# Forward substitution of a delta rule by finished rows, with its matrix and products in PSUM

## The chip, the cores and the metric

The kernel runs on one core of one Trainium2 chip. The metric is the device time of one execution in microseconds, as the median of several runs. The engines are named as the profile names them: PE (TensorE, the matmuls; PEld are its weight loads), DVE (VectorE), ACT (ScalarE), POOL (GpSimd) and SP (SyncE, which issues the DMAs). PSUM is the memory that PE writes its products to; SBUF is the other memory of the core.

## The reference, cut to what matters

A network of three blocks on 512 tokens of 1024 features (and 256 context tokens in the first two). The third block has, beside a dilated attention, a gated delta rule with 8 heads of 128 features, worked in 4 chunks of 128 tokens. Inside a chunk the rule needs the solution of a triangular system:

```
L[t, s] = beta_t * exp(g_t - g_s) * (k_t . k_s)     for s < t, else 0
T       = (I + L)^-1                                per head and chunk, 128 x 128
u       = T (beta v),   w = T (beta exp(g) k)
```

Here g is the running sum of the log decays. u and w then go through a scan over the four chunks of a head, which carries a state of 128 x 128.

## The kernel before, in words

The delta rule (`delta`, L1290) takes the 8 heads in two groups of four. For each group it runs five steps:

1. `delta_prep` (L1140), once for each head: loads q, k and v from a DRAM scratch, norms q and k, makes the decays, and leaves in SBUF the matrix L as `Lm` (four chunks, L1185) and the other factors. The normed keys and queries are in a tile `kq`, three buffers for all heads.
2. `delta_base` (L1200): the inverses of the 32 x 32 blocks on the diagonal of I + L. There are 4 heads x 4 chunks x 4 blocks = 64 of them. They are written to DRAM (L1207) and read back so that each block lies in a partition of its own (`Lb`, [64, 32, 32], L1209). DVE changes the sign (L1210), sets `Tb` to the unit matrix (L1212, L1213) and then works row by row: for row i, one product of row i of -L with the first i rows of T, read transposed (L1217), and one sum over the last axis, which gives row i of T (L1218). Both have i x i elements in each of 64 partitions; i runs from 1 to 31, and each instruction needs the one before it. The result goes to DRAM (L1219). `Lb`, `Tb` and the products are in buffers of `kq`.
3. `delta_merge` (L1221), for each head: loads the blocks back onto the diagonal of a 128 x 128 matrix (`Tz`, L1244), transposes it on PE (L1237), and joins 32-blocks to 64 and 128 with matmuls (L1231), DVE subtractions from PSUM (L1256) and ACT copies from PSUM (L1246, L1252, L1255, L1258).
4. `delta_scan` (L1261): the scan over the chunks, four heads side by side.
5. The norm of the outputs (L1308 to L1313).

Between the groups `fill` is called: the projections of the dilated attention, matmuls of 512 columns (L140 to L142) with weights that are loaded by SP (L127), split by ACT (L133) and POOL (L134) into two parts, and results that ACT and, where a gate is formed, DVE (L1043) take out of PSUM and SP stores (L1044). They depend on nothing in the delta rule. More projections (`fill1` in `second`, L1438) are called behind the dilated attention, which follows the delta rule.

The instructions are not run in the order of the program text. A planner goes through the whole program when it is built; each engine takes, of the instructions whose inputs are ready in its plan, the one that comes first in the text (unless a priority is changed). The times of the plan are the planner's own. So projections that stand later in the text are put between the steps of a group wherever PE would have nothing to do in the plan. On the chip each engine runs its instructions in the planned order and waits, at each, for what it needs; the DMA queue of SP likewise.

Two pools of PSUM matter. `pm` has three buffers of 512 fp32 values in each partition, tag "mm", for the projections. `ps` has five of this size, tag "sm", for all small products of the delta rule and later of the attention. Buffers of a tag are taken in turn, and a tile waits until the last reader of the buffer's former tile is done.

Of the kernel before, what the change touches and what calls it, by code (L numbers as in the profile page):

```python
# [29 lines left out]
class Group:  # L30
    """Latent (0) or context (1) tokens: residual x and split activations, both feature-major."""
# [6 lines left out]
class Tiles:  # L38
    """Feature tiles [P, 8, m], the first six in one buffer and the last two in another."""
# [14 lines left out]
class Core:  # L54
# [14 lines left out]
    def weights(self, stack, NR, NW, first=0):  # L69
        """More weight buffers for a phase: NR raw loads of 2048 columns, NW splits of 1024; first is the raw one to start at."""  # L70
        pool = stack.enter_context(self.tc.tile_pool(name=self.nm("wp"), bufs=1, reuse_waits="tile"))
        for kind, n in (("wr", NR), ("wh", NW), ("wl", NW)):
            old = self.wbufs.get(kind, [])
            self.wbufs[kind] = old + [(pool, f"{kind}{len(old) + i}") for i in range(n)]
            stack.callback(self.wbufs.__setitem__, kind, old)
        self.wi = {"wr": first - 1}
        stack.callback(self.wi.clear)

    def wt(self, kind, shape, dt=F32):
        """The next weight buffer in turn."""  # L80
# [11 lines left out]
    def exp_table(self):  # L92
        """Behind the silus traced so far, the activation table that has both exp and ln."""
# [10 lines left out]
    def feat(self, pool, g, tag):  # L104
        """Split activations of a group."""
# [3 lines left out]
    # ---------------------------------------------------------------- weights  # L109
# [13 lines left out]
    def wcols(self, w, c0, engs=None):  # L123
        """256 columns of a [1024, *] matrix as two splits [P, 8, 128]."""
# [19 lines left out]
    def gemm(self, ps, w, H, L):  # L144
        """ps[128, n] = w.T @ (H + L) over the feature tiles."""
# [9 lines left out]
    def sigm(self, out, x):  # L155
        """out = 1 / (1 + exp(-x)) with the functions of one activation table."""
# [5 lines left out]
    def vgemm(self, pt, g, i, w, cs):  # L162
        """pt[128 tokens of tile i, 256] = h.T @ w, token-major; w: two splits of four feature tiles."""
# [6 lines left out]
    def wrows(self, w, c0):  # L170
        """256 columns of a [1024, *] matrix as two splits [P, 4 * 256] of four feature tiles."""
# [4 lines left out]
    # ---------------------------------------------------------------- setup  # L176
# [21 lines left out]
    def conditions(self, ps, pp):  # L198
        """silu of the three condition vectors, feature-major."""
# [8 lines left out]
    def params(self, ps, pp):  # L208
        """Small vectors, laid feature-major by PE transposes."""
# [18 lines left out]
    def matvec(self, ps, sb, i0, w, c0, ncol, bias, dst, tag="mv"):  # L228
        """dst[p, tile, :] = (cond[i0:i0+2] @ w[:, c0:c0+ncol])[tile*128+p] + bias, feature-major; yields after each load.
        The products add up in PSUM where the tag is mv, in SBUF where its buffers are shared."""  # L230
# [26 lines left out]
    def matvec_dve(self, ps, sb, n, w, c0, bias, dst, tag):  # L257
        """The same for 2048 / n columns and the first n conditions, the products added up by VectorE; only the sums over
        the partitions are left to TensorE."""
# [37 lines left out]
    def tick(self, n=1):  # L297
        """Advance the products that run beside a phase by n loads."""
# [7 lines left out]
    def later(self, n, f, *args):  # L306
        """f traced with its priority lowered by n instructions."""
# [5 lines left out]
    # ---------------------------------------------------------------- norm  # L313
    def affine(self, g, mod, shift, scale, i):
        """Gain and shift of a modulated norm: per-partition scalars of the 8 feature tiles."""
# [4 lines left out]
    def rstd(self, out, ps, inv):  # L320
        """out = (ps * inv + eps) ** -0.5"""
# [5 lines left out]
    def norm(self, ps, groups, mods, tag="sm"):  # L327
        """H + L = modulated norm of x, split."""
# [31 lines left out]
    # ---------------------------------------------------------------- ffn  # L360
    def ffn_w(self, w_in, c):
        """256 columns each of gate and up."""
        return self.wcols(w_in, c * 256), self.wcols(w_in, FFN + c * 256)

    def ffn(self, ps, sb, groups, gates, w_in, w_out, ticks, pre):
        """x += gate * (silu(h w_gate) * (h w_up)) w_out; ticks: loads beside each of so many chunks; pre: the first ffn_w."""
# [32 lines left out]
    # ---------------------------------------------------------------- tokens in  # L399
# [46 lines left out]
class Even(Core):  # L446
    def even_setup(self, cp, ps):
# [22 lines left out]
        # lower bounds: softmax over the two layers, first row  # L470
# [25 lines left out]
    # ------------------------------------------------------------ attention  # L496
    def qk_norm(self, ps, sb, pl, pc, gain, out):
        """out[128 = two heads x 64, 768]: head norm with gain, rope on the latent columns."""
# [18 lines left out]
    def attend(self, ps, sb, q, k, vt, t, i, yq):  # L517
        """Query tile i of heads t and 4 + t."""
# [28 lines left out]
        # exponentials, their sums with the sink's  # L547
# [15 lines left out]
        # token-major products with the values  # L563
# [20 lines left out]
    # ------------------------------------------------------------ hgrn  # L584
    def hgrn_dir(self, sb, d, h, pl, pc):
        """Gates of one direction: 1 - f and the cumulative log f inside chunks of 128."""
# [13 lines left out]
    def hgrn_part(self, ps, sb, d, q, k, cum, c0, m):  # L600
# [26 lines left out]
        # keys of the half of a chunk that comes first, queries of the other, from the bound between them  # L627
# [19 lines left out]
        # scores [s, t] by blocks of 32 keys; the parts that are masked whole are left out  # L647
# [61 lines left out]
    # ------------------------------------------------------------ mixer  # L709
    def even_mixer(self, groups, ydram, side, out):  # L710
# [3 lines left out]
        with tc.tile_pool(name="ev", bufs=1, reuse_waits="tile") as sb, tc.tile_pool(name="evmm", bufs=2, space=PSUM, reuse_waits="tile") as pm, \  # L714
# [17 lines left out]
            def pair(c0, c1):  # L732
                """Two 128-column tiles of w_in."""
# [10 lines left out]
            # keys and values of the attention  # L744
# [4 lines left out]
            # each of the two heads with zeros in place of the other  # L749
# [15 lines left out]
            # values of the recurrence, token-major  # L765
# [9 lines left out]
            for hd in range(4):  # L775
# [18 lines left out]
                # attention heads hd and 4 + hd  # L794
# [18 lines left out]
    def even_out_a(self, pm, sb, groups, pools, gates, ydram, xdram, ys):  # L813
        """x += gate * y w_out over the first three heads of each kind, x in DRAM; y takes the place of the split
        activations, and the last two feature tiles of these stage the loads until ys, the last heads, fill them."""
# [38 lines left out]
    def even_out_b(self, ps, groups, gates):  # L854
        """The rest: the last head of each kind."""
# [41 lines left out]
class Odd(Even):  # L897
    def odd_mixer(self, groups, gate, pre):
# [3 lines left out]
        with tc.tile_pool(name="od", bufs=1, reuse_waits="tile") as sb, tc.tile_pool(name="odmm", bufs=2, space=PSUM, reuse_waits="tile") as pm, \  # L902
# [39 lines left out]
            for hd in range(4):  # L942
# [15 lines left out]
                # values, token-major  # L958
# [8 lines left out]
                # scores with decay, times the values  # L967
# [15 lines left out]
                # head norm, gate  # L983
# [45 lines left out]
class Second(Odd):  # L1029
    def gemm_store(self, pm, sb, wt, g, dst, func, scale=1.0, dil=1):  # L1030
        """One 128-column tile of a projection through an activation to a DRAM scratch, tokens by class mod dil."""
# [25 lines left out]
    # ------------------------------------------------------------ delta rule  # L1057
    def betas_w(self, sb, w):
        """The 16 columns of the beta and decay projections, split."""
# [7 lines left out]
    def betas_in(self, pm, sb, g, wt, dst):  # L1067
        """Their products, feature-major, to a DRAM scratch."""
# [6 lines left out]
    def betas(self, pm, sb, bad):  # L1075
        """Token-major beta and decay scalars, [128 tokens, 4 chunks, 8 heads]."""
# [18 lines left out]
        # log1p(e) = ln(u) + (e - (u - 1)) / u, u = 1 + e rounded  # L1095
# [24 lines left out]
    def conv(self, pt, y, r):  # L1120
        """Causal depthwise convolution over 4 tokens, silu; feature tile r of q, k, v."""
# [7 lines left out]
    def conv_store(self, pm, sb, g, w, dst):  # L1129
        """Convolved q, k, v tiles of all heads to a DRAM scratch."""  # L1130
# [9 lines left out]
    def delta_prep(self, ps, sb, hd, cd):  # L1140
# [17 lines left out]
        # decays  # L1158
# [17 lines left out]
        # products inside the chunks  # L1176
# [10 lines left out]
        # token-major keys and values  # L1187
# [12 lines left out]
    def delta_base(self, sb, heads, ld, td):  # L1200
        """Inverses of the 32-blocks of I + L on the diagonal, by forward substitution, a block per partition."""
# [8 lines left out]
        nc.vector.tensor_scalar(Lb, Lb, -1.0, None, ALU.mult)  # L1210
# [3 lines left out]
        tmp = self.T(sb, [n, 32, 32], "kq", bufs=3)  # L1214
        Tt = Tb.rearrange("p r e -> p e r")
        for i in range(1, 32):
# [539 lines left out]
```

## Time and profile before

| what | us |
|---|---|
| median of 3 runs | 3058.72 |
| lowest and highest run | 3056.5, 3059.95 |
| span of the profiled execution | 3050.9 |
| PE busy in it | 2816.8 (92%) |
| DVE busy | 1429.2 (47%) |
| ACT busy | 1052.4 (34%) |
| POOL busy | 991.3 (32%) |

The span runs from the first to the last instruction of the profiled execution; no other time is given for that execution, and the runs were 5.6 to 9.1 us longer than its span, the median 7.8 us. PE's busy time counts matmuls that overlap, so a high share does not mean that PE is at its peak. Times in the views are microseconds from the start of the span.

### The profile page before, as it was taken

What the parts mean: (1) busy time and instruction counts of PE and PEld (TensorE: products, weight loads), DVE (VectorE), ACT (ScalarE), POOL (GpSimd) and SP (SyncE); (2) the same over time, 40 slices, a digit from 0 to 9 for tenths busy, and PEclk for the clock granted to TensorE, in tenths of its full rate; (3) what the DMA queues carried; (4) which work ended last, traced back from release to release, by engine and by line L of the source; (5) the groups of instructions that cost most, each with busy time, mean ns of one, the idle gap of its engine ahead of it and who ended that gap; (6) DMA issues with size and microseconds to landing.
All of it is one profiled execution on the core that took longest, in us unless ns stands there. A gap on an engine that the chain in (4) does not pass through costs nothing. (4 is left out here: it accounts for less than half of the span.)

```text
span 3050.9 us, 38015 instructions
## 1 busy us (share of the span) xinstructions
PE 2816.8 (92%) x15400; PEld 2297.4 (75%) x15400; DVE 1429.2 (47%) x2190; ACT 1052.4 (34%) x1916; POOL 991.3 (32%) x498
## 2 busy tenths in 40 slices
PE   6988988988999999999999999999999979979898
PEld 4866767767888888788888866777768768758677
DVE  6265556574644233633233243333354573672555
ACT  4244434342112121423323243222244524635533
POOL 2221121133223232325243334444334332322443
PEclk7999989999999999999999999999999989989999
DMA  7222132363332121212122214222244431433622
GB/s 264 70 82 82 35 106 71 92 233 111 101 134 97 56 69 56 76 55 83 55 83 69 66 73 165 83 97 97 83 146 158 153 116 65 138 92 106 213 78 89
DMA packets 220823, 312.67 MB, mean 102 GB/s; under 512 B 27430, under 2 KB 172360, under 8 KB 214120
## 3 DMA queue, kind: packets, MB, share of 16 engines
q1 hardware_dynamic: 220648, 310.25, 30.8%
q8 instruction: 121, 1.98, 0.3%
q14 instruction: 54, 0.44, 0.0%
HBM read 275.31 MB, written 34.90 MB: 102 GB/s over the span
## 5 line engine op out<-in xcount | busy, mean ns | idle before, releaser
L134 POOL TENSOR_TENSOR wl<-wr,wh 128x1024 fp32r<-128x1024 f32 x200 | 489.0, 2447 | 938.3 <-ACT wh L133 912.9
L140 PE MATMUL mm<-hH,wh 128*128 128x512 f32 x1760 | 707.9, 403 | 15.7 <-ACT hH L354 7.0
L141 PE MATMUL mm<-hL,wh 128*128 128x512 f32 x1760 | 706.2, 401 | 9.4 <-POOL hL L352 8.3
L142 PE MATMUL mm<-hH,wl 128*128 128x512 f32 x1760 | 703.6, 400 | 0.0
L133 ACT ACTIVATE wh<-wr 128x1024 fp32r<-128x1024 f32 x200 | 211.4, 1058 | 603.0 <-PE mm L141 475.9
L140 PEld LDWEIGHTS mm<-hH,wh 128*128 128x128 f32 x1760 | 335.9, 191 | 97.9 <-ACT hH L354 11.2
L141 PEld LDWEIGHTS mm<-hL,wh 128*128 128x128 f32 x1760 | 335.2, 190 | 89.1 <-POOL hL L352 12.8
L120 POOL TENSOR_TENSOR wl<-wr,wh 128x1024 fp32r<-128x1024 f32 x96 | 236.4, 2465 | 507.6 <-ACT wh L119 506.1
L142 PEld LDWEIGHTS mm<-hH,wl 128*128 128x128 f32 x1760 | 335.8, 191 | 73.1 <-issue 4.7
L358 DVE SCALAR_TENSOR_TENSOR xl<-mm,modT,xl 128x512 f32<-128x512 f32 x216 | 160.4, 749 | 151.1 <-PE mm L142 143.8
L381 DVE TENSOR_TENSOR sg<-mm,sg 128x512 f32<-128x512 f32 (+1 forms) x66 | 39.7, 601 | 405.3 <-PE mm L142 405.3
L141 PE MATMUL mm<-aL,wh 128*128 128x512 f32 (+1 forms) x528 | 194.0, 368 | 32.5 <-DVE aL L153 32.5
L140 PE MATMUL mm<-aH,wh 128*128 128x512 f32 (+1 forms) x528 | 190.7, 367 | 3.9 <-ACT aH L152 3.9
L142 PE MATMUL mm<-aH,wl 128*128 128x512 f32 (+1 forms) x528 | 190.7, 365 | 0.0
L141 PE MATMUL mm<-cL,wh 128*128 128x256 f32 x640 | 185.0, 289 | 0.7 <-POOL cL L352 0.7
L140 PE MATMUL mm<-cH,wh 128*128 128x256 f32 x640 | 183.9, 287 | 1.7 <-ACT rsg L914 1.7
L142 PE MATMUL mm<-cH,wl 128*128 128x256 f32 x640 | 183.7, 287 | 0.0
L119 ACT ACTIVATE wh<-wr 128x1024 fp32r<-128x1024 f32 x96 | 100.9, 1053 | 142.4 <-PE mm L141 83.3
L141 PEld LDWEIGHTS mm<-aL,wh 128*128 128x128 f32 x528 | 102.6, 194 | 54.8 <-DVE aL L153 39.4
L153 DVE TENSOR_TENSOR aL<-sg,aH 128x512 fp32r<-128x512 f32 (+1 forms) x66 | 111.6, 1690 | 44.4 <-ACT aH L152 44.4
L141 PEld LDWEIGHTS mm<-cL,wh 128*128 128x128 f32 x640 | 123.1, 192 | 7.9 <-issue 4.2
L140 PEld LDWEIGHTS mm<-cH,wh 128*128 128x128 f32 x640 | 123.2, 192 | 5.2 <-ACT rsg L914 2.1
(489 smaller groups left out, 5215.5 us busy)
## 6 DMA issues: line engine op xcount, KB each, us to landing
wr<-in_mod_w_dram SPq DMA_DIRECT2D x48, 1024.0 KB, 7.0
wr<-in_ffn_w_in_dram SPq DMA_DIRECT2D x44, 1024.0 KB, 5.1
wr<-in_w_in_dram SPq DMA_DIRECT2D x36, 1024.0 KB, 5.6
wr<-in_odd_w_in_dram SPq DMA_DIRECT2D x24, 1024.0 KB, 5.0
wr<-in_ffn_w_out_dram SPq DMA_DIRECT2D x22, 1024.0 KB, 5.3
wr<-in_ada_w_dram SPq DMA_DIRECT2D x12, 1024.0 KB, 5.0
wr<-in_even_w_in_dram SPq DMA_DIRECT2D x18, 512.0 KB, 4.3
wr<-in_odd_w_out_dram SPq DMA_DIRECT2D x8, 1024.0 KB
```

Source lines behind the costliest of these rows:

```text
L119: self.nc.scalar.activation(H, rv, AF.Copy)
L120: self.nc.gpsimd.tensor_tensor(L, rv, f32(H), ALU.subtract)
L133: self.nc.scalar.activation(H, v, AF.Copy)
L134: (engs[j] if engs else self.nc.gpsimd).tensor_tensor(L, v, f32(H), ALU.subtract)
L140: mm(out, lH, rH, start=first, stop=False, **kw)
L141: mm(out, lH, rL, start=False, stop=False, **kw)
L142: mm(out, lL, rH, start=False, stop=last, **kw)
L153: (eng or self.nc.gpsimd).tensor_tensor(L, src, f32(H), ALU.subtract)
L358: self.nc.vector.scalar_tensor_tensor(g.x[:, m_, :], po, gate[:, m_:m_ + 1], g.x[:, m_, :], ALU.mult, ALU.add)
L381: nc.vector.tensor_tensor(sg, pu, sg, ALU.mult)
```

## The change

`delta_base` gets the pool `ps` of small PSUM tiles as an argument. Two ACT copies with scale -1 take the place of DVE's scaling and put -L into two PSUM tiles, `Lp`, of 16 rows each. The loop no longer makes one row at a time out of all rows above it; it takes each finished row j from all rows below it. For j from 0 to 30 the products of column j of -L (rows j+1 to 31) with row j of T (its first j+1 elements) go to a PSUM tile `tmp`, by one instruction for each half of L that has such rows, and one instruction adds them to these rows of `Tb`, in place in SBUF. `tmp` is a tile of its own for each j. The third `kq` buffer, for the products, is no longer taken. The result is the same up to the order of the sums.

```diff
-    def delta_base(self, sb, heads, ld, td):
+    def delta_base(self, ps, sb, heads, ld, td):
...
         Lb = self.T(sb, [n, 32, 32], "kq", bufs=3)
         nc.sync.dma_start(Lb, ld.rearrange("h c b r e -> (h c b) r e"))
-        nc.vector.tensor_scalar(Lb, Lb, -1.0, None, ALU.mult)
+        Lp = [self.T(ps, [P, 512], "sm")[:n].rearrange("p (r e) -> p r e", e=32) for _ in range(2)]
+        for i in range(2):
+            nc.scalar.activation(Lp[i], Lb[:, 16 * i:16 * i + 16, :], AF.Copy, scale=-1.0)
         Tb = self.T(sb, [n, 32, 32], "kq", bufs=3)
         nc.vector.memset(Tb, 0.0)
         nc.vector.memset(Tb.rearrange("p r e -> p (r e)")[:, 0:1024:33], 1.0)
-        tmp = self.T(sb, [n, 32, 32], "kq", bufs=3)
-        Tt = Tb.rearrange("p r e -> p e r")
-        for i in range(1, 32):
-            nc.vector.tensor_tensor(tmp[:, :i, :i], Lb[:, i:i + 1, :i].to_broadcast([n, i, i]), Tt[:, :i, :i], ALU.mult)
-            nc.vector.tensor_reduce(Tb[:, i, :i], tmp[:, :i, :i], AX.X, ALU.add)
+        for j in range(31):
+            w = j + 1
+            tmp = self.T(ps, [P, 512], "sm")[:n]
+            done = 0
+            for i in range(2):
+                r0, r1 = max(w, 16 * i), 16 * i + 16
+                if r0 >= r1:
+                    continue
+                m = r1 - r0
+                nc.vector.tensor_tensor(tmp[:, done * w:(done + m) * w].rearrange("p (r e) -> p r e", e=w),
+                                        Lp[i][:, r0 - 16 * i:r1 - 16 * i, j:j + 1].to_broadcast([n, m, w]),
+                                        Tb[:, j:j + 1, :w].to_broadcast([n, m, w]), ALU.mult)
+                done += m
+            nc.vector.tensor_tensor(Tb[:, w:, :w], tmp[:, :done * w].rearrange("p (r e) -> p r e", e=w), Tb[:, w:, :w], ALU.add)
         nc.sync.dma_start(td.rearrange("h c b r e -> (h c b) r e"), Tb)
...
-            self.delta_base(sb, heads, ld, td)
+            self.delta_base(ps, sb, heads, ld, td)
```

## Rows read from the trace of the kernel before

**Rows 1.** The page, part 1: busy us of each engine, share of the span, instructions

```profile
PE 2816.8 (92%) x15400; PEld 2297.4 (75%) x15400; DVE 1429.2 (47%) x2190; ACT 1052.4 (34%) x1916; POOL 991.3 (32%) x498
```

**Rows 2.** Waits of PE, 2380 to 2850: engine, line, releaser: us in total, times, longest

```profile
PE sm L1237 <- DMA Tz<-td: 38.6, 2, 20.1
```

**Rows 3.** Timeline of PE: start us, us, engine, line, operation [idle before it <-releaser]

```profile
2440.76 0.48 PE L141 MATMUL mm<-hL,wh 128*128 128x512 f32 x1
...
2492.31 0.39 PE L140 MATMUL mm<-hH,wh 128*128 128x512 f32 x1
2512.78 1.09 PE L1237 MATMUL sm<-ident,Tz 128*128 128x128 f32 x4 [20.08 <-DMA Tz<-td]
```

**Rows 4.** Timeline of DVE, substitution of the first group

```profile
2451.12 0.70 DVE L1210 TENSOR_SCALAR kq<-kq 64x1024 f32<-64x1024 f32 x1 [5.13 <-DMA kq<-ld]
...
2452.50 0.16 DVE L1217 TENSOR_TENSOR kq<-kq,kq 64x4 f32<-64x4 f32 x1
2452.69 0.15 DVE L1218 TENSOR_REDUCE kq<-kq 64x2 f32<-64x4 f32 x1
...
2454.12 2.38 DVE L1217 TENSOR_TENSOR kq<-kq,kq 64x36 f32<-64x36 f32 x1
...
2505.09 1.15 DVE L1218 TENSOR_REDUCE kq<-kq 64x31 f32<-64x961 f32 x1
```

**Rows 5.** Timeline of DVE, substitution of the second group, its ends

```profile
2666.69 2.39 DVE L1210 TENSOR_SCALAR kq<-kq 64x1024 f32<-64x1024 f32 x1 [3.53 <-DMA kq<-ld]
...
2674.24 0.67 DVE L1043 TENSOR_TENSOR st<-st,mm 128x512 f32<-128x512 f32 x1
...
2722.16 1.15 DVE L1218 TENSOR_REDUCE kq<-kq 64x31 f32<-64x961 f32 x1
```

**Rows 6.** Groups of DVE by form, 2451 to 2507: shape, count | busy us, mean ns

```profile
L1217 DVE TENSOR_TENSOR kq<-kq,kq 64x961 f32<-64x961 f32 x1 | 1.8, 1789 | 0.0
...
L1218 DVE TENSOR_REDUCE kq<-kq 64x31 f32<-64x961 f32 x1 | 1.1, 1146 | 0.0
...
L1217 DVE TENSOR_TENSOR kq<-kq,kq 64x1 f32<-64x1 f32 x1 | 0.2, 153 | 0.1
...
L1218 DVE TENSOR_REDUCE kq<-kq 64x1 f32<-64x1 f32 x1 | 0.1, 147 | 0.2 <-DVE kq L1217 0.2
```

**Rows 7.** Timeline of POOL, weight splits beside the substitution

```profile
2454.03 2.39 POOL L134 TENSOR_TENSOR wl<-wr,wh 128x1024 fp32r<-128x1024 f32 x1 [2.75 <-ACT wh L133]
2459.48 2.40 POOL L134 TENSOR_TENSOR wl<-wr,wh 128x1024 fp32r<-128x1024 f32 x1 [3.06 <-ACT wh L133]
```

**Rows 8.** Timelines of POOL and DVE in the scan, a stretch of both

```profile
2568.70 2.37 POOL L134 TENSOR_TENSOR wl<-wr,wh 128x1024 fp32r<-128x1024 f32 x1 [14.00 <-ACT wh L133]
...
2569.27 0.35 DVE L1287 SCALAR_TENSOR_TENSOR S<-S,gl,sm 128x128 f32<-128x128 f32 x1 [0.82 <-PE sm L1282]
```

**Rows 9.** Timeline of DVE in the scalars of the delta rule, 32 elements

```profile
2395.17 0.19 DVE L1100 TENSOR_TENSOR be<-be,bu 128x32 f32<-128x32 f32 x1
...
2397.42 0.19 DVE L1115 TENSOR_TENSOR bed<-mm,bgc 128x32 f32<-128x32 f32 x1 [0.23 <-PE mm L1112]
```

**Rows 10.** Timeline of ACT in the merge, a copy

```profile
2517.32 0.60 ACT L1252 ACTIVATE t<-sm 128x512 f32<-128x512 f32 x1 [2.82 <-PE sm L1231]
```

**Rows 11.** Stretches: us, busy us of PE, PEld, DVE, ACT, POOL, granted clock, DMA, GB/s

```profile
2513.00:2517.00 4.00, 4.00 (x17) 3.62 (x16) 0.00 (x0) 0.60 (x1) 0.00 (x0) 0.50 0.72 195
...
2730.00:2737.00 7.00, 7.00 (x30) 6.25 (x31) 0.01 (x1) 1.20 (x2) 0.05 (x1) 0.59 0.72 196
2577.00:2610.00 33.00, 31.71 (x131) 24.05 (x130) 7.39 (x8) 21.29 (x34) 11.33 (x5) 1.00 0.37 120
2800.00:2950.00 150.00, 136.38 (x738) 106.04 (x736) 72.40 (x128) 77.66 (x212) 55.68 (x34) 0.99 0.46 150
```

**Rows 12.** Timeline of SP, DMAs issued between the groups

```profile
2611.25 0.32 SPq L1146 DMA_DIRECT2D cy<-cd  x1
2612.00 0.32 SPq L1044 DMA_DIRECT2D zd<-st  x1
```

## The prediction

> **What bounds the kernel now.** I read the waits of TensorE first, then its busy time by stretches, then the timelines of the two places that the waits name. The run is TensorE's nearly throughout [rows 1], so a shorter VectorE chain is worth only the TensorE time that it sets free. Around the delta rule that time is in one kind of wait: twice the first transpose of the merge (L1237) waits for the blocks that come back from DRAM, 38.6 us in all, the longer 20.1 us, so the other 18.5 [rows 2]. The reader is to see next that these waits are not a lack of work. TensorE runs the filling projections from 2440.76, behind the last transposes of the preparation, to 2492.31 plus 0.39, and then stands before an instruction whose input arrives at 2512.78 [rows 3]. Its queue is in the order that the planner fixed when the program was built: 52 us of projections were placed where 72 us passed.
>
> The 72 us are VectorE's substitution. From the scaling at 2451.12 to the end of the last sum, 2505.09 plus 1.15, it takes 55.1 us in the first group [rows 4]; 56.6 in the second (2666.69 to 2722.16 plus 1.15) [rows 5]. Its instructions tell why it is longer than its size. The sums follow 0.147 us plus 1.04 ns an element ((1146-147)/960), but the products 0.153 us plus 1.70 ns, for their second input is read down a column [rows 6]. Start to start, the smallest take 0.19 us [rows 4]. So 31 products and 31 sums of 10,416 elements each are 62 x 0.19 + 10,416 x (1.70 + 1.04) ns = 11.8 + 28.5 = 40.3 us; 54.3 passed between 2451.93 and the end. The other 14 us are in products that take some 2 us too long: 36 elements took 2.38 us [rows 4] where the slope gives 0.21. It starts inside a GpSimd weight split from 2454.03 to 2456.42 and ends when that does [rows 7]. Eight of the 31 products of the group are held so.
>
> **The change, part by part.** *The substitution.* For each j there are 31-j rows of j+1 elements: 5,456 products and as many sums, half of before. Rows in both halves of L (j up to 14) need two products: 15 x 2 + 16 = 46 products, 31 sums, 77 instructions. At 0.19 us each and 1.04 ns an element this is 14.6 + 11.4 = 26.0 us. The slope is that of the sums because no input runs down a column within a row any more (the column of L is one value per row, held while the row runs).
>
> *The hold by GpSimd.* Each product now has one input in PSUM and one in SBUF, each sum too. Such instructions are not held: inside the weight split from 2568.70 to 2571.07 a VectorE instruction with one input in each, and its output in SBUF, took 0.35 us [rows 8]. I take the hold as gone, 0 us; if it stays, see the third rival.
>
> *The price of PSUM.* No instruction of VectorE writes PSUM in this trace, so this is bounded. Reading it costs nothing: 32 elements take 0.19 us with an input in PSUM and 0.19 with both in SBUF [rows 9]. Below, 0, or some 0.1 us less where two products of a step follow each other without a wait, 1.5 us a group; above, one more fixed part of 0.15 us on each of 77, 11.6 us a group. I take 0, by the read. The Trainium skill, Perfetto Trace Analysis, section "Optimizing Scalar/DVE Operations", speaks against the change: some 60 ns of overhead for a VectorE access to SBUF, 125 to PSUM. By it the sum would be 77 x 65 ns = 5 us a group dearer; the equal rows don't bear it out for reads, and no row shows it for writes.
>
> *The scaling.* One VectorE instruction goes (0.70 us in the first group, 2.39 in the second, where it too was held [rows 4, 5]); two ScalarE copies of 64 x 512 come, at most the 0.60 us of its 128 x 512 copy [rows 10], so 1.2 us. They stand in ScalarE's queue between weight splits that wait for TensorE to free a buffer; ahead of one they are on time, behind one they are some 3 us late, for the one beside L's arrival at 2451.12 let GpSimd go on at 2454.03 [rows 4, 7]. I take 1.0 between 0 and 3. The splits behind the copies serve tiles after the next, so a few us there cost nothing; if they were late by more than the 5.4 us from one split to the next [rows 7], TensorE would wait the rest.
>
> *The buffers.* L's halves hold two of the five PSUM buffers of the small products, the steps rotate through the other three; nothing else uses them while the substitution runs, for the projections have their own. One SBUF buffer of the normed keys comes free; what could use it, the second group's preparation, waits for TensorE. These cost 0. The DMAs are the same in number and size. Evacuations of projections on VectorE stay: three in the second group's stretch, 0.67 us each [rows 5].
>
> *The chain* is then 1.2 + 1.0 + 26.0 = 28.2 us for 55.1, and 28.2 + 1.3 (two of the evacuations) for 56.6: 27 us shorter in each group.
>
> *What TensorE gets of it.* That depends on the planner's new order. Its 52 us of projections fit 72 us less the 55.1 of the chain (16.9) plus 35 for the substitution. Its old instructions at 1.04 ns an element and without holds are 0.8 + 11.8 + 20,832 x 1.04 ns = 34.3: it priced neither the columns nor GpSimd. By the same price the new ones are 1.2 + 14.6 + 11.4 = 27.2, so it will place some 7 us fewer projections. The waits become 20.1 - 27 + 7 = 0, and 18.5 - 27 + 7, below zero: none. I leave 1.5 us each for the ScalarE copies. What is late next is the projections themselves.
>
> *The clock.* Behind both waits TensorE ran at its lower level: granted 0.50 (1.2 GHz) from 2513 to 2517 and 0.59 from 2730 to 2737, where long busy stretches show 1.00 [rows 11]. That is 4 x 0.50 + 7 x 0.41 = 4.9 us. Without idle stretches it does not fall; I keep 0.5 us as lost.
>
> *The projections not placed.* In the first group they run later, all of them before the second group is prepared: the first input of that is fetched at 2611.25, as the last result of this filling is stored, 2612.00 [rows 12], and TensorE is busy 31.7 of the 33 us ahead [rows 11]. So there TensorE sets the time and gains what it no longer waits. In the second they go to the attention stage, which has 13.6 us of idle TensorE in 150 [rows 11]; 7 us find room.
>
> **Sum:** 38.6 + 4.9 - 3.0 - 0.5 = 40 us. The profiled execution has a span of 3050.9 us and the median of the runs is 7.8 us above, which lies around the span in both; 3058.7 - 40 = **3019 us**.
>
> **The rivals.**
> 1. *The planner takes the fill away* (0.13). If it shortens the placed projections by most of what the chain gains, TensorE waits as long as before, only earlier, and the projections come later. At worst the first group gains nothing, and the second the idle time of the attention stage that its 20 to 27 us of projections can fill, some 7 of 13.6 us: 3052. Half of it, 9 us of wait in each group and half the clock, is 3058.7 - 20 - 2.5 = 3036. For it: the order is fixed beforehand and changes with any price. Against: its 52 us fit the price that gives only 7.
> 2. *PSUM is dear to VectorE* (0.10). At 0.15 us more on each of 77 the chain gains 15 us, the waits are 12 and 10 us, and half the clock stays lost: 3058.7 - 16.6 - 2.5 = 3040. Nothing in the trace shows such a write; the equal reads speak against. This is where the page's rule belongs: with 5 us a group the waits would be 5 and 3 us, the time about 3026.
> 3. *The hold stays* (0.06), so that the change does only half of what it says. A split occupies 2.4 of every 5.4 us [rows 7]; five or six would catch an instruction in 28 us, at the 2 us of before 11 us a group. The waits are then 11 and 9 us: 3039, or 3046 with the clock still falling. The instruction inside a split [rows 8] speaks against.
> 4. *Slower* (0.06). One mechanism: each step writes PSUM and the next instruction must see it, a trip that the chain makes 77 times a group. From 27/77 = 0.35 us more for each instruction the chain is longer than now; at 0.5 us it is 11.5 us longer in each, while the planner has placed 7 us less: 3058.7 + 37 = 3096 at most. The reads from PSUM at 0.19 us leave no sign of such a trip.
> 5. *No change that can be seen* (0.05): the new order gives back elsewhere, in the attention stage, what the waits gave: 3053 to 3064.
>
> **How the numbers follow.** The forecast has 0.60, from 3007 (no wait left, and the attention stage's idle time filled for 7 us besides) to 3034. Rivals 1 to 3 reach to 3046 with most of their 0.29; the range is 3007 to 3044. A measurement of this kernel can tell 0.2%, 6 us, from no change. Faster by more: 0.60 and nearly all of 0.29, 0.88; within it 0.06; slower 0.06.
>
> **What would show it.** In the changed profile: VectorE's groups on the three new lines, 46 and 31 a group, with the smallest at 0.15 to 0.19 us and none near 2.4; the stretch from the first product to the last sum 26 to 29 us; TensorE's wait for the merge's blocks at a few us instead of 38.6; the granted clock at 1.00 behind it. A wait that stays with a short chain would make rival 1 right; small instructions of 0.3 us, rival 2; long ones beside a GpSimd split, rival 3. I am wrong outright if the chain comes out as long as before, or if it shortens and the attention stage lengthens by as much.

## The result: 1.6% faster, TensorE's wait for the blocks gone

The changed kernel takes 3009.15 us (median of 4 runs, 3007.48 to 3013.4) where the kernel before took 3057.61 us in the runs beside it (3052.31 to 3059.95): a ratio of 0.9843 [0.9831, 0.9856], 48.5 us less. The forecast was 3019, 3007 to 3044. Between the two profiled executions the span fell by 45.5 us, 3050.9 to 3005.4.

The page of the kernel after, its first line and PE's line of part 1, answers to [rows 1]:

```profile
span 3005.4 us, 38050 instructions
...
PE 2810.6 (94%) x15400; PEld 2288.8 (76%) x15400; DVE 1372.2 (46%) x2218; ACT 1053.6 (35%) x1920; POOL 986.4 (33%) x498
```

These two lines and [rows 1] split the gain. Span less busy time is what PE stands idle: 3050.9 - 2816.8 = 234.1 us before, 3005.4 - 2810.6 = 194.8 after, so 39.3 us of the gain are idle time; the other 6.2 are busy time, the same 15,400 matmuls at a mean granted clock of 0.973 where it was 0.967. The idle time is nearly all one wait, 37.9 us of it. Waits of PE after, 2380 to 2850 (engine, line, releaser: us in total, times, longest), the answer to [rows 2], where 38.6 us stood:

```profile
PE sm L1249 <- DMA Tz<-td: 0.7, 2, 0.4
```

That wait was VectorE's substitution. The timeline of DVE after, first group (start us, us, engine, line, operation, idle before it), the answer to [rows 4]:

```profile
2456.21 0.17 DVE L1226 TENSOR_TENSOR sm<-sm,kq 64x15 f32<-64x15 f32 x1 [5.42 <-ACT sm L1213]
2456.86 0.17 DVE L1226 TENSOR_TENSOR sm<-sm,kq 64x16 f32<-64x16 f32 x1 [0.47 <-ACT sm L1213]
2457.07 0.21 DVE L1230 TENSOR_TENSOR kq<-sm,kq 64x31 f32<-64x31 f32 x1
2457.31 0.41 DVE L1226 TENSOR_TENSOR sm<-sm,kq 64x28 f32<-64x28 f32 x2
...
2470.62 0.42 DVE L1226 TENSOR_TENSOR sm<-sm,kq 64x256 f32<-64x256 f32 x1
2471.08 0.42 DVE L1230 TENSOR_TENSOR kq<-sm,kq 64x256 f32<-64x256 f32 x1
...
2482.37 0.18 DVE L1230 TENSOR_TENSOR kq<-sm,kq 64x31 f32<-64x31 f32 x1
```

From 2456.21 to 2482.55 it is 26.3 us (in the second group 28.0, with three evacuations of projections in between). The largest product and the largest sum, 256 elements, take 0.42 us each. The 0.47 us in front of the second product are a wait for the second of ACT's two copies, which stand in ACT's timeline as one row:

```profile
2455.58 1.11 ACT L1213 ACTIVATE sm<-kq 64x512 f32<-64x512 f32 x2 [1.82 <-DMA kq<-ld]
```

The groups of both substitutions after show the means, and what POOL did meanwhile shows that nothing is held: the weight splits still run every 5.4 us beside the products, and the longest of the 92 products of the whole run takes 0.425 us.

```profile
L1226 DVE TENSOR_TENSOR sm<-sm,kq 64x60 f32<-64x60 f32 (+14 forms) x92 | 25.9, 281 | 13.1 <-ACT sm L1213 10.2
L1230 DVE TENSOR_TENSOR kq<-sm,kq 64x31 f32<-64x31 f32 (+15 forms) x62 | 20.7, 334 | 2.1
```

```profile
2464.30 2.40 POOL L134 TENSOR_TENSOR wl<-wr,wh 128x1024 fp32r<-128x1024 f32 x1 [3.06 <-ACT wh L133]
2469.72 2.40 POOL L134 TENSOR_TENSOR wl<-wr,wh 128x1024 fp32r<-128x1024 f32 x1 [3.02 <-ACT wh L133]
```

The first fence is the lines view of DVE from 2430 to 2700 (busy us, mean ns, idle before), the second POOL's timeline. The product at 2470.62 and the sum at 2471.08 run at their usual length inside the split that lasts from 2469.72 to 2472.12.

One part got longer, behind the loop. The timelines of SP and PE after:

```profile
2482.58 0.47 SPq L1231 DMA_DIRECT2D td<-kq  x1
2486.49 0.33 SPq L1044 DMA_DIRECT2D vd<-st  x1
2488.49 0.38 SPq L127 DMA_DIRECT2D wr<-in_w_in_dram  x1
2488.92 6.29 SPq L1256 DMA_DIRECT2D Tz<-td  x8
```

```profile
2445.55 0.48 PE L141 MATMUL mm<-hL,wh 128*128 128x512 f32 x1
...
2495.08 0.39 PE L140 MATMUL mm<-hH,wh 128*128 128x512 f32 x1
2495.74 0.63 PE L1249 MATMUL sm<-ident,Tz 128*128 128x128 f32 x4 [0.27 <-DMA Tz<-td]
```

The blocks are sent off at 2482.58, but in SP's order a store of a projection and a weight load stand ahead of the loads that bring them back, so PE's transposes start 13.2 us behind the last sum, where before it was 6.5 (2506.24 to 2512.78 in [rows 4] and [rows 3]). It costs nothing here, for PE has projections up to 2495.47: the wait in front of the transposes is 0.27 us. And behind them the clock holds: the granted clock is 1.00 where [rows 11] show 0.50 behind the first wait (behind the second, 0.59 there, the kernel after has 1.00 from 2650 to 2770). Stretches after, first group (us, busy us of PE, PEld, DVE, ACT, POOL, granted clock, DMA share, GB/s):

```profile
2493.00:2513.00 20.00, 19.50 (x121) 15.77 (x121) 4.27 (x7) 7.62 (x11) 4.66 (x5) 1.00 0.33 99
2513.00:2577.00 64.00, 63.68 (x392) 52.40 (x392) 21.88 (x43) 30.84 (x58) 14.93 (x8) 1.00 0.21 69
```

### The profile page after: what moved, and what is told of

Same layout as the page of the kernel before. It is cut to its first block, busy times and chain, and to the rows that moved or that the text cites. A ratio compares the mean times of both kernels' runs of the same rounds, so it can differ in the third digit from the quotient of the medians.

```text
span 3005.4 us, 38050 instructions
## 1 busy us (share of the span) xinstructions
PE 2810.6 (94%) x15400; PEld 2288.8 (76%) x15400; DVE 1372.2 (46%) x2218; ACT 1053.6 (35%) x1920; POOL 986.4 (33%) x498
## 5 line engine op out<-in xcount | busy, mean ns | idle before, releaser
L140 PE MATMUL mm<-hH,wh 128*128 128x512 f32 x1760 | 705.8, 402 | 12.9 <-ACT hH L354 7.1
L141 PE MATMUL mm<-hL,wh 128*128 128x512 f32 x1760 | 704.4, 400 | 10.0 <-POOL hL L352 8.9
L142 PE MATMUL mm<-hH,wl 128*128 128x512 f32 x1760 | 700.6, 398 | 0.0
L140 PEld LDWEIGHTS mm<-hH,wh 128*128 128x128 f32 x1760 | 334.4, 190 | 94.0 <-ACT hH L354 11.5
L141 PEld LDWEIGHTS mm<-hL,wh 128*128 128x128 f32 x1760 | 334.2, 190 | 89.8 <-POOL hL L352 13.7
L142 PEld LDWEIGHTS mm<-hH,wl 128*128 128x128 f32 x1760 | 334.4, 190 | 72.8 <-issue 4.4
L141 PE MATMUL mm<-aL,wh 128*128 128x512 f32 (+1 forms) x528 | 194.9, 369 | 32.9 <-DVE aL L153 32.9
L140 PE MATMUL mm<-aH,wh 128*128 128x512 f32 (+1 forms) x528 | 191.1, 367 | 4.0 <-ACT aH L152 4.0
L142 PE MATMUL mm<-aH,wl 128*128 128x512 f32 (+1 forms) x528 | 191.0, 365 | 0.0
L141 PE MATMUL mm<-cL,wh 128*128 128x256 f32 x640 | 184.9, 289 | 0.9 <-POOL cL L352 0.9
L140 PE MATMUL mm<-cH,wh 128*128 128x256 f32 x640 | 183.9, 287 | 1.7 <-ACT rsg L914 1.7
L142 PE MATMUL mm<-cH,wl 128*128 128x256 f32 x640 | 183.7, 287 | 0.0
L141 PEld LDWEIGHTS mm<-aL,wh 128*128 128x128 f32 x528 | 102.9, 195 | 55.2 <-DVE aL L153 39.7
L141 PEld LDWEIGHTS mm<-cL,wh 128*128 128x128 f32 x640 | 123.0, 192 | 8.0 <-issue 4.2
L140 PEld LDWEIGHTS mm<-cH,wh 128*128 128x128 f32 x640 | 123.2, 193 | 5.4 <-ACT rsg L914 2.2
```

The costliest lines, as they stand in the source:

```text
L140: mm(out, lH, rH, start=first, stop=False, **kw)
L141: mm(out, lH, rL, start=False, stop=False, **kw)
L142: mm(out, lL, rH, start=False, stop=last, **kw)
```

## The experiments

The theory: the gain is the end of a wait, the wait is the part of VectorE's chain that the planner did not price, and that part is mostly the holds by GpSimd, which go because every instruction has one input in PSUM. The rivals: that the halved work alone does it, that only the planner's order matters, or that one of the two PSUM operands is enough. The kernel before, measured again beside each experiment, had medians of 3056.92 to 3059.23 us, so medians of different rows compare to some 2 us. "Loop" below is the time from the first product to the end of the last sum in the first group, "wait" PE's wait for the blocks in both groups, "idle" span less PE's busy time.

| kernel | loop, us | wait, us | idle, us | median, us |
|---|---|---|---|---|
| before, profiled execution | 54.3 | 38.6 | 234.1 | 3058.7 |
| order only | 57.7 | 32.3 | 233.7 | 3057.89 |
| new loop, all in SBUF | 36.9 | 23.0 | 221.4 | 3043.36 |
| new loop, only products in PSUM | 37.3 | 21.0 | 217.7 | 3038.05 |
| new loop, only L in PSUM | 35.3 | 18.6 | 213.0 | 3032.6 |
| old loop, L in PSUM | 41.7 | 14.7 | 211.9 | 3027.48 |
| after | 26.3 | 0.7 | 194.8 | 3009.15 |
| no substitution | 0 | 0.6 | 188.0 | 3003.87 |
| new loop, twice | 53.6 | 0.6 | 221.8 | 3054.75 |

### The new loop without PSUM

The new order of the work, with -L made by VectorE and left in SBUF and the products in SBUF:

```diff
-        Lp = [self.T(ps, [P, 512], "sm")[:n].rearrange("p (r e) -> p r e", e=32) for _ in range(2)]
-        for i in range(2):
-            nc.scalar.activation(Lp[i], Lb[:, 16 * i:16 * i + 16, :], AF.Copy, scale=-1.0)
+        nc.vector.tensor_scalar(Lb, Lb, -1.0, None, ALU.mult)
+        Lp = [Lb[:, 16 * i:16 * i + 16, :] for i in range(2)]
...
-            tmp = self.T(ps, [P, 512], "sm")[:n]
+            tmp = self.T(sb, [P, 512], "dtmp", bufs=3)[:n]
```

> The changed loop (finished rows, half the elements), but L and the products in SBUF: VectorE scales L in place as before, each product and each sum has two SBUF inputs. Theory (the gain is the TensorE wait, and the hold by GpSimd is what PSUM takes away): every instruction of the loop can now be held, about 2.2 us in each 5.4 us, so the 26 us become 38 to 44; TensorE waits some 15 to 20 us a group again and the time is 3040 to 3056, most of the gain lost although the elements are halved. Rival (the halved elements and the rows without a column make the gain, PSUM is incidental): the loop stays at 26 to 30 us, the waits at a few us, the time at 3009 to 3015.

Measured: 3043.36 us, 0.9953 [0.9937, 0.997]. The timelines of DVE and POOL of this kernel:

```profile
2456.77 0.34 DVE L1225 TENSOR_TENSOR dtmp<-kq,kq 64x48 f32<-64x48 f32 x2
...
2457.44 2.44 DVE L1225 TENSOR_TENSOR dtmp<-kq,kq 64x55 f32<-64x55 f32 x2
...
2462.65 2.69 DVE L1225 TENSOR_TENSOR dtmp<-kq,kq 64x63 f32<-64x63 f32 x2
...
2468.10 2.63 DVE L1229 TENSOR_TENSOR kq<-dtmp,kq 64x240 f32<-64x240 f32 x1
```

```profile
2457.19 2.47 POOL L134 TENSOR_TENSOR wl<-wr,wh 128x1024 fp32r<-128x1024 f32 x1 [2.75 <-ACT wh L133]
2462.64 2.40 POOL L134 TENSOR_TENSOR wl<-wr,wh 128x1024 fp32r<-128x1024 f32 x1 [2.98 <-ACT wh L133]
2468.07 2.40 POOL L134 TENSOR_TENSOR wl<-wr,wh 128x1024 fp32r<-128x1024 f32 x1 [3.02 <-ACT wh L133]
```

Six instructions of the first group are held, one to each split, whether product or sum, and each ends within 0.3 us of its split. The loop loses some 13 us so. Half the elements and no column reads are worth 15 us of the time; the place of L and of the products has the other 34, in part through the planner, as the last part of the next section shows.

### The old loop with L in PSUM

```diff
-        nc.vector.tensor_scalar(Lb, Lb, -1.0, None, ALU.mult)
+        Lp = [self.T(ps, [P, 512], "sm")[:n].rearrange("p (r e) -> p r e", e=32) for _ in range(2)]
+        for i in range(2):
+            nc.scalar.activation(Lp[i], Lb[:, 16 * i:16 * i + 16, :], AF.Copy, scale=-1.0)
...
-            nc.vector.tensor_tensor(tmp[:, :i, :i], Lb[:, i:i + 1, :i].to_broadcast([n, i, i]), Tt[:, :i, :i], ALU.mult)
+            nc.vector.tensor_tensor(tmp[:, :i, :i], Lp[i // 16][:, i % 16:i % 16 + 1, :i].to_broadcast([n, i, i]), Tt[:, :i, :i], ALU.mult)
```

> The old loop (product and sum of all rows above, columns read, all elements), with only L in two PSUM tiles, copied there by ScalarE; the products stay in SBUF. Theory: the products have one SBUF input each and are not held, the sums never were; the loop takes 40 to 42 us instead of 54, the waits of TensorE fall from 38.6 to some 10 us together, and the time is 3017 to 3026: about three quarters of the gain from the place of L alone. Rival (elements make the gain): the loop shortens by less than 5 us and the time is over 3045.

Measured: 3027.48 us, 0.9902 [0.9887, 0.9917], 1.5 us above the top of the range expected: 31 us of the gain, with the old products merely reading one input from elsewhere (and the scaling, 0.7 and 2.4 us before, taken off VectorE). Lines of DVE, old products before (L1217, 2430 to 2730) and in this kernel (L1219, 2430 to 2720):

```profile
L1217 DVE TENSOR_TENSOR kq<-kq,kq 64x1 f32<-64x1 f32 (+30 forms) x62 | 71.7, 1157 | 2.2
```

```profile
L1219 DVE TENSOR_TENSOR kq<-sm,kq 64x1 f32<-64x1 f32 (+30 forms) x62 | 48.1, 776 | 11.8 <-ACT sm L1212 9.7
```

The same 62 products cost 23.6 us less, and the longest is 1.95 us, that of 961 elements; none is held. The sums, which have one input each, were never held and cost the same 30.7 us in both.

### One of the two operands in PSUM

First L alone (the products in SBUF), then the products alone (L in SBUF): the edits are the last two lines and the first five of the diff of the new loop without PSUM.

> The new loop with L's two halves in PSUM and the products written to SBUF: every product has one input in PSUM and one in SBUF, every sum has both in SBUF. Theory (an instruction of VectorE with both inputs in SBUF stands still while a GpSimd weight split runs, and one split holds exactly one instruction, whichever comes first): each of the five or six splits beside the loop still catches one instruction, now always a sum, for 2.0 to 2.4 us; so the sum's line shows several at 2.3 to 2.7 us, the product's line none over 0.45, the loop takes 35 to 38 us in the first group, nearly the 36.9 of the loop all in SBUF, and the time is 3032 to 3046. Rival (the loss goes with the number of instructions that can be held, so half of them cost half): the loop takes 30 to 33 us, and the time is 3018 to 3028. Rival (the place of the products does not matter): the loop takes 26 us, and the time is 3007 to 3014.

> The reverse: L is scaled by VectorE and stays in SBUF, the products are written to PSUM: every product has both inputs in SBUF and its output in PSUM, every sum one input in each. Theory (the inputs decide, not the output): the holds stand on the product's line alone, at 2.3 to 2.9 us, one to a split, none on the sum's line over 0.45; the loop takes 35 to 38 us in the first group, the time is 3032 to 3048. If an output in PSUM alone were enough, no instruction would be held, the loop would take 26 to 28 us, and the time would be 3007 to 3016. If half of the instructions cost half, the loop is 30 to 33 us and the time 3018 to 3030.

Measured: 3032.6 us, 0.9912 [0.9896, 0.9927], and 3038.05 us, 0.9925 [0.9909, 0.9942]. Timelines of DVE, with only L in PSUM and, in the next fence, with only the products there; a split started at 2468.74 in the one and at 2470.07 in the other:

```profile
2461.65 0.28 DVE L1226 TENSOR_TENSOR dtmp<-sm,kq 64x28 f32<-64x28 f32 x2
...
2468.29 0.43 DVE L1226 TENSOR_TENSOR dtmp<-sm,kq 64x63 f32<-64x63 f32 x2
2468.76 2.62 DVE L1230 TENSOR_TENSOR kq<-dtmp,kq 64x207 f32<-64x207 f32 x1
2471.41 0.44 DVE L1226 TENSOR_TENSOR dtmp<-sm,kq 64x60 f32<-64x60 f32 x2
```

```profile
2463.21 0.41 DVE L1225 TENSOR_TENSOR sm<-kq,kq 64x28 f32<-64x28 f32 x2
...
2469.99 0.33 DVE L1229 TENSOR_TENSOR kq<-sm,kq 64x175 f32<-64x175 f32 x1
2470.36 2.52 DVE L1225 TENSOR_TENSOR sm<-kq,kq 64x64 f32<-64x64 f32 x2
2472.91 0.35 DVE L1229 TENSOR_TENSOR kq<-sm,kq 64x192 f32<-64x192 f32 x1
```

With L in PSUM only sums are held, six of them in the first group; with the products there only products, again six; none of the other kind is longer than 0.42 us. It is the inputs that decide: two in SBUF are held, one in each memory is not, and an output in PSUM doesn't help. And the loss doesn't halve with the number of instructions that can be held: a split catches the first one that comes, and with a product and a sum in turn one always comes. The loops are 35.3 and 37.3 us, beside 36.9 with all in SBUF, so both operands in PSUM are needed and the first buys next to nothing of the loop. (The times are still 11 and 5 us under that of the loop all in SBUF; that is the planner's doing, see the end of the next section.) The Trainium skill states the rule for the inputs (SBUF — State Buffer, section "SBUF: two separate sides": VectorE and GpSimd share a pair of ports, which a VectorE operation with two SBUF inputs locks against a GpSimd operation that reads SBUF, and the loser waits); these traces agree, at 1.6 to 2.3 us lost per split of 2.4, and the other way round the splits beside the old loop's long products, which often run when a split starts, take up to 3.41 us.

The first row of each fence shows the price of a write to PSUM that the prediction had to bound. Two products of one step don't depend on each other; written to SBUF they overlap and take 0.28 us together, written to PSUM 0.41. Taking the holds out, the loop is 23.9 and 24.2 us where the products go to SBUF and 26.0 and 26.3 where they go to PSUM: 2.1 us a group, 15 pairs at some 0.13. An instruction by itself costs nearly the same either way, 0.17 to 0.18 us against 0.16 to 0.17 at 15 or 16 elements.

### The order alone

The kernel before, with the first transposes of the first group's merge tied behind the first matmul of a later tile of the projections, so that PE has more to do in front of them:

```diff
+            if k == 0:
+                self.tiles.append(mm.ins.name)
...
+                t = nc.tensor.transpose(pt[:, c * P:(c + 1) * P], src[:, c, :], self.ident)
+                self.first = self.first or t.ins
...
+                self.tc.add_manual_dep(self.first, self.tiles[16], mybir.DependencyInfo(mybir.DependencyClass.NoSync, mybir.DependencyReason.DATA), reason="order")
```

> The kernel before with nothing changed but TensorE's order in the first group: the first transpose of the merge is put behind the first matmul of the 17th tile of the filling projections, some 3 to 4 tiles (about 20 us) later than the planner put it. VectorE's loop is the old one, 54 us. Theory (the kernel loses TensorE time, not VectorE time): the 20.1 us wait of the first group goes, the second stays at 18.5, and the time falls by 18 to 23 us, to 3035 to 3040, without a shorter chain. Rival (the length of the chain sets the end): no change, 3055 to 3060, the projections only move.

Measured: 3057.89 us, 1.0001 [0.9991, 1.001]: missed. Timelines of PE and ACT of this kernel:

```profile
2520.64 1.08 PE L1241 MATMUL sm<-ident,Tz 128*128 128x128 f32 x4 [8.58 <-DMA Tz<-td]
...
2529.81 2.07 PE L1235 MATMUL sm<-U,t 128*128 128x128 f32 x8 [6.38 <-ACT U L1251]
```

```profile
2528.22 1.06 ACT L134 ACTIVATE wh<-wr 128x1024 fp32r<-128x1024 f32 x1 [8.98 <-DMA wr<-in_w_in_dram]
2529.18 0.58 ACT L1251 ACTIVATE U<-sm 128x512 f32<-128x512 f32 x1
```

The first wait fell from 20.1 to 8.6 us, but more splits beside the loop held more of it (57.7 us), the loads of the blocks came later still, and the copy that the merge needs first stood in ACT's queue behind a split whose weights had not come: a new wait of 6.4. In the second group the wait rose from 18.5 to 23.8. 8.6 + 6.4 + 23.8 = 38.8: the wait was moved, not removed. Since the edit lengthened the loop too, it doesn't settle what a well-placed order could give the kernel before; that stays open.

### No substitution, and the substitution twice

Two ends. The first has `for j in range(0)` in place of `range(31)`; the second runs the two memsets and the loop twice (`for again in range(2):` around them).

> The changed kernel with the loop left out (31 products and sums a group): the blocks stay unit matrices. The loads, the scaling, the store and the merge stay. Theory (TensorE no longer waits here, so a still shorter chain is worth nothing): 3003 to 3012, within 0.2% of the changed kernel. Rival (the chain still sets the end): 26 us a group less, so 2957 to 2975.

> The changed kernel with its substitution run twice in a row on the same blocks (cleared again in between), which gives the same blocks: 26 to 28 us more of VectorE per group, none of it held. The chain is then about as long as before the change, but the planner knows its length: it places 137 more projections in the first group's stretch, 122 more in the second's. Theory (TensorE's wait was the part of the chain that the planner did not price, holds and column reads, not its length): the wait of the merge's first transposes stays under 6 us in all, the substitution lasts 53 to 56 us in the first group, no instruction of it over 0.6 us, and the time is 3010 to 3040, what it loses lying behind the second group's merge, where the projections that were taken forward are missing. Rival (the chain's length sets the wait, as in the kernel before): the wait comes back to 30 us or more, and the time is over 3045.

Measured without it: 3003.87 us, 0.9826 [0.9812, 0.9841], as expected: the last 26 us of each group's chain are worth some 5 us (the interval overlaps that of the kernel after), because PE doesn't wait for them any more.

Measured with it twice: 3054.75 us (3045.55 to 3068.7, 10 runs), 0.9991 [0.9976, 1.0007]. Half of the theory held. The loop is 53.6 us, as long as before the change, and the wait is 0.6 us where the kernel before had 38.6: this chain, which the planner priced at no less than it takes (the sum is at the end of the next section), isn't waited for, though it is as long as the old one. The time was missed by 15 us. Waits of PE from 2380 to 2850 and two stretches of this kernel:

```profile
PE sm L1340 <- DMA dv<-vd: 9.1, 1, 9.1
PE sm L1323 <- ACT csq L1321: 8.5, 3, 2.9
...
PE sm L1250 <- DMA Tz<-td: 0.6, 1, 0.6
```

```profile
2770.00:2800.00 30.00, 22.70 (x158) 18.73 (x156) 9.33 (x28) 8.96 (x24) 0.00 (x0) 0.97 0.07 26
2800.00:2835.00 35.00, 18.32 (x55) 11.50 (x55) 6.51 (x14) 9.71 (x26) 3.42 (x3) 0.50 0.44 150
```

The projections were taken forward to cover the longer chains, and behind the second merge there are none left: in 65 us PE stands idle for 24 and runs at half the clock in the end of it, waiting for the norm of the outputs and the first tiles of the attention, which had been covered. The same stretch behind the second merge of the kernel after, 2724.6 to 2789.6, has 2 us of idle time, so this is 22 of the 27 us more idle time; 23 us more are busy time, at a mean granted clock of 0.963 against 0.973.

## Why the prediction was right

In the main the forecast's mechanism is what happened, and its price was 10 us too careful. Two of its terms, the chain and the planner, were each some 5 us off and offset each other. By its steps:

- *The loop*: 26.0 us forecast from 77 instructions at 0.19 us and 1.04 ns an element; 26.3 measured, 0.47 of it the wait for the second copy.
- *The hold* taken as gone: it is, and the two runs with one operand in PSUM show why. The row it was read from [rows 8] had one input in each memory, as the new instructions have. (The eight holds of before were not all "some 2 us": by the prediction's own slope they cost 1.1 to 2.2 us each, 13.4 together.)
- *The price of PSUM* taken as 0 between -1.5 and +11.6: an instruction by itself pays nothing, but pairs lose the overlap that they have in SBUF, 2.1 us a group. The prediction had the other side of this, a gain of 1.5 us that it left out of its sum, so the sum stood. The estimate from the page's figures (the Trainium skill, Perfetto Trace Analysis, "Optimizing Scalar/DVE Operations") was 5 us; the runs show less than half of it, and only where two writes follow each other without a wait.
- *The scaling*, 2.2 us with its lateness: the first product starts 0.63 us after the copies do (2455.58 to 2456.21) and they started as L came. The copies were on time; with the second product's 0.47 they cost the chain 1.1 us.
- *The chain*, 27 us shorter: from the first projection behind the preparation to the merge's first transpose it went from 72.0 us (2440.76 to 2512.78) to 50.2 (2445.55 to 2495.74), by 21.8. The loop and the scaling give 28; SP's queue behind the loop takes 6.7 back. This term was not in the prediction, which took the way through DRAM as unchanged because "the DMAs are the same in number and size". Their place in SP's order isn't.
- *The planner*, 7 us fewer projections placed: PE's fill in front of the first merge went from 51.9 us (2440.76 to 2492.70) to 49.9 (2445.55 to 2495.47), by 2 us. That is 9 matmuls fewer, 219 for 228. The kernels at the two ends show why: without the loop 80 stand there, with the loop twice 356. So the planner places 139 and 137 matmuls for one loop, some 31 us at 0.228 us each, where the prediction priced it at 26.0. The two misses cancel: 20.1 - 21.8 + 2.0 = 0.3, where the prediction had 20.1 - 27 + 7 = 0.1 and left 1.5. Both fit a plan in which the loop ends 5 us later than it did, but no run tells whether SP's order comes from that; as far as the runs go, that the two offset each other is luck.
- *The residue* of 3.0 us: 0.7. *The clock*, 4.4 us gained: 6.2 us less busy time in all.
- *The sum*: 40 us forecast, 45.5 between the spans, 39.3 of idle and 6.2 of busy time. The rest of the 10 us is in the step to the median: "7.8 us above, which lies around the span in both" was wrong. Each later run lists its own span, and lies some 2 us above it (3009.15 beside spans of 3005.4 to 3011.3). By that, the profiled execution of before took some 3053 us, one of its shorter ones, 5 us under the median: what lay between its span and the median was mostly the spread of the runs and no constant.
- Two side sums don't come out as written. Rival 3's waits of 11 and 9 us leave 18.6 of the 38.6, so 3040 with the clock still falling and some 2.5 us less with half of it back, not 3046 and 3039; and the terms of the low end, 38.6 + 4.9 + 7 = 50.5, give 3008 and not 3007. The result doesn't hang on either.

Of the rivals, the one that said the planner takes the fill away came nearest to being needed: it did not happen here, but the doubled loop shows that its other side is real, for projections taken forward are missing later. Dear PSUM, a hold that stays and a slower round trip through PSUM show no sign in the 92 products, of which none is over 0.43 us.

The table also corrects a picture that the prediction used only in part. The wait doesn't follow the length of the loop: 41.7 us of the old loop leave 14.7 us of wait, 35.3 us of the new one 18.6, and 53.6 of the doubled one 0.6. It follows what the planner didn't count, here the holds, and in the old loop the columns too. This can be worked out from the projection matmuls (L140 to L142) that PE has between the last transposes of the preparation and the first of the merge. A third of them are of L141; its lines in that stretch of the first group, for the kernel before, the new loop all in SBUF, the kernel after and the kernel without the loop:

```profile
L141 PE MATMUL mm<-hL,wh 128*128 128x512 f32 x76 | 29.7, 391 | 0.0
L141 PE MATMUL mm<-hL,wh 128*128 128x512 f32 x60 | 23.4, 390 | 0.0
L141 PE MATMUL mm<-hL,wh 128*128 128x512 f32 x73 | 28.5, 391 | 0.0
L141 PE MATMUL mm<-hL,wh 128*128 128x512 f32 x27 | 10.6, 393 | 0.0
```

Without the loop there are 80 in all. What stands there beyond 80, at 0.228 us each (49.9 us for the 219 of the kernel after), is an estimate of the planner's price of the loop:

| kernel | matmuls | priced, us | took, us | took less priced | first wait, us |
|---|---|---|---|---|---|
| before | 228 | 33.7 | 54.3 | 20.6 | 20.1 |
| new loop, all in SBUF | 180 | 22.8 | 36.9 | 14.1 | 13.8 |
| new loop, only products in PSUM | 195 | 26.2 | 37.3 | 11.1 | 10.2 |
| new loop, only L in PSUM | 194 | 26.0 | 35.3 | 9.3 | 8.0 |
| old loop, L in PSUM | 230 | 34.2 | 41.7 | 7.5 | 7.0 |
| after | 219 | 31.7 | 26.3 | -5.4 | 0.3 |
| new loop, twice | 356 | 62.9 | 53.6 | -9.3 | 0.6 |

Where the loop takes longer than its price, the difference is the wait to within 1.3 us (in the second group, worked out in the same way from the 84 there, to within 3.2); where it takes less, there is no wait to speak of. So PSUM took the wait away in two ways. Nothing is held, which makes the real loop 10.5 us shorter than the one in SBUF; and the planner prices instructions on PSUM higher, which put 39 more matmuls, 8.9 us, in front of the merge. The second belongs to the planner and not to the chip. It is also why one operand in PSUM gained time without shortening the loop (14 and 15 more matmuls in the first group, 21 and 22 in the second), and why the new loop with only L in PSUM is shorter than the old one with L there and still 5 us slower (194 for 230).

## What to carry to other kernels

On VectorE beside a GpSimd that reads SBUF, look for instructions that end when GpSimd's do: give every one of a dependent chain an input in PSUM, for one kind left in SBUF is caught as often as two. Where an order is fixed beforehand, a wait is the difference between the planned and the real length of a chain, so first remove what the plan can't know (holds, strides), then what it can; and count what the plan placed before crediting the chip, for a changed price moves work too. Independent work that covers a chain is a budget: what is placed there is missing at the next gap, so a shorter chain is worth its wait and no more once the wait is gone.

## What was not expected of the hardware

- Two independent VectorE products of 28 to 32 elements in 64 partitions, one behind the other, take 0.28 us together with SBUF outputs and 0.41 with PSUM outputs; a single one of 15 or 16 elements takes 0.16 to 0.17 and 0.17 to 0.18.
- A product of 961 elements whose one input is a row in PSUM and whose other is read down columns of SBUF takes 1.95 us, against 1.79 with both in SBUF [rows 6]; without the column, no such difference was seen (256 elements, 0.42 us in every place).
- A GpSimd split of 2.4 us beside a chain of short VectorE instructions holds exactly one of them, for 1.6 to 2.3 us (first groups), and isn't itself slowed by more than 0.3 us; beside the old loop, whose products take up to 1.8 us, a split takes up to 3.41 us.
